# Attention queries and keys: turning by VectorE's 32x32 squares and a round trip through DRAM in place of TensorE transposes

## The chip, the cores and the metric

The kernel runs on one core of one Trainium2 chip. The metric is the device time of one execution in microseconds (us); lower is better. The engines are named as in the profile: PE is TensorE (PEld its weight loads), DVE is VectorE, ACT is ScalarE, POOL is GpSimd, and SP is SyncE, which issues nearly all the DMAs.

## The reference, cut to what matters

The program is a trunk of two layers over 1024 tokens of width 1024. Layer 0 mixes tokens by a gated MLP and a gated delta rule, layer 1 by differential attention; each layer then has an MLP and a gate. Everything is float32. The change concerns the attention of layer 1 alone:

```python
def diff_attention(qkv, q_gain, k_gain, lam_params, sub_gain, lam_init):
    q, k, v = jnp.split(qkv, 3, axis=-1)          # 8 heads, 2 branches of 64 each
    q = rms_norm(q.reshape(bsz, seq, C_HEADS, 2, C_HEAD_DIM), q_gain) * (C_HEAD_DIM ** -0.5)
    k = rms_norm(k.reshape(bsz, seq, C_HEADS, 2, C_HEAD_DIM), k_gain)
    ...
        logits = jnp.einsum('bqhrd,bkhrd->bhrqk', q_blk, k) - slopes * dist
        logits = jnp.where(dist >= 0, logits, -jnp.inf)
        probs = jax.nn.softmax(logits, axis=-1)
        attn = probs[:, :, 0] - lam * probs[:, :, 1]
        return jnp.einsum('bhqk,bkhe->bqhe', attn, v)
```

The projections give q and k with tokens on partitions. The product of q and k sums over features, so both must be turned to features on partitions first.

## The kernel before

The function `attention` works head by head (8 heads, each with two branches of 64 features, so 128 features) and in each head by 8 blocks of 128 queries.

**Projections.** A stream of units (`proj_qk`, `proj_v`) computes q, k and v; each weight is split into a high and a low float32r part (L223 on ACT, L224 on POOL here), and each product takes three matmuls. `proj_qk(hd, qk)` yields, for each of four pairs of token tiles `t2`, a PSUM tile with 256 tokens of q and k. Its `evac` squares it (L914, ACT), reduces it (L916, DVE), takes the power -1/2 (L919, POOL), and `scale` (L923, DVE) writes q and k, normalised, to the SBUF tiles `qk[0]` and `qk[1]`: each a pair of tiles of 128 partitions (tokens) by 4 x 128 (four token tiles by 128 features), one for each half of the sequence. `scale` runs one unit after the `evac` that made it.

**Turning.** `put_k(hf)` turns half `hf` of k by four PE transposes into a PSUM tile `pt`, and writes it from there with the gain to `ks`, as a float32r high part (L969, ACT) and the rest (L970, DVE), for each branch. `put_q(b2)` does the same for 256 queries with two transposes (L980 on ACT, L981 and L982 on DVE). `begin(hd + 1)` calls `put_k(0)` and `put_q(0)` of the next head towards the end of this one; `put_k(1)` follows in the head's own block 2 or 3, and `put_q` before each further pair of blocks.

**Blocks.** For each block and branch, two matmuls give the logits (qk, L76), one DVE operation adds the position term and finds the running minimum (L1016), ACT takes the exponential (L1019), DVE combines the two branches (L1027), PE transposes the result to PSUM (tr), ACT copies it out (aT, L1037), and PE multiplies it with v (po). The outputs go to `o_dram` on SP (L1065).

**The order.** The loop over the blocks runs the steps of three successive blocks beside each other, and calls `pump()` four times for each block; `pump` takes units of the projection stream (and at the end of the output product) by a table of marks. The framework then orders each engine's instructions by a planner that works with estimated times, and sets the waits; every engine takes its queue in that order. Weight loads (L101) go through 8 raw buffers on SP's queue. All PE instructions show as L76 (matmul) or L79 (transpose), as a helper records them.

Of the kernel before, what the change touches and what calls it, by code (L numbers as in the profile page):

```python
# [11 lines left out]
F32 = mybir.dt.float32  # L12
# [6 lines left out]
P = 128  # L19
# [4 lines left out]
HT = 512  # L24
# [15 lines left out]
def f32(ap):  # L40
    return ap.bitcast(F32)
# [73 lines left out]
class Trunk:  # L115
# [756 lines left out]
    def attention(self, w_qkv, w_out, gain_next, h_dram):  # L872

        nc = self.nc
        NB = NT
        hs, r = list(self.hs), list(self.r)
# [16 lines left out]
        def proj(label, srcs, t2s, evac):  # L893
            def units(w):
                for t2 in t2s:
                    ps = self.mm_ps()
                    for i in range(2):
                        h, c = tok(2 * t2 + i)
                        for k in range(KT):
                            self.mm3(ps[:, 256 * i : 256 * (i + 1)], [x[:, c] for x in hs[h][k]], w.at(k), k == 0, k == KT - 1)  # L900
                            if k == 3 or (k == 7 and i == 0):
                                yield None
                    yield evac(t2, ps)

            n = 256 // len(srcs)
            return Proj(label, [(ap, i * n) for i, ap in enumerate(srcs)], 256, units, 4 * len(t2s), nc.gpsimd)

        def proj_qk(hd, qk):
            def evac(t2, ps):
                if not qk:  # L910
                    qk.append([self.slot(f"c{2 * (hd % 2) + i}", [P, 4, P], F32, "q") for i in range(2)])
                    qk.append([self.slot(f"c{4 + i}", [P, 4, P], F32, "k") for i in range(2)])
                sq = self.tmp()
                nc.scalar.activation(sq, ps, AF.Square)  # L914
                ss = self.sp.tile([P, 2, 4], F32, tag="ss", name=self.nm("ss"))
                nc.vector.tensor_reduce(ss, sq.rearrange("p (t g d) -> p t g d", t=2, g=4), AX.X, ALU.add)  # L916
                nc.vector.scalar_tensor_tensor(ss, ss, 1.0 / 64, e2[:, 2 * t2 : 2 * t2 + 2].unsqueeze(2).to_broadcast([P, 2, 4]), ALU.mult, ALU.add)
                f = self.sp.tile([P, 8], F32, tag="ssf", name=self.nm("ssf"))
                nc.gpsimd.tensor_tensor(f, ss.rearrange("p t g -> p (t g)"), self.mhalf[:, 0:8], ALU.pow)  # L919

                def scale():
                    for i in range(2):
                        nc.vector.tensor_tensor(  # L923
                            qk[i][t2 // 2][:, 2 * (t2 % 2) : 2 * (t2 % 2) + 2, :].rearrange("p t (g d) -> p t g d", d=64),
                            ps.rearrange("p (t i g d) -> p t i g d", t=2, i=2, d=64)[:, :, i],
                            f.rearrange("p (t i g) -> p t i g", t=2, i=2)[:, :, i].unsqueeze(3).to_broadcast([P, 2, 2, 64]), ALU.mult)

                return scale

            return proj(f"qk{hd}", [w_qkv[:, i * D + hd * P : i * D + (hd + 1) * P] for i in range(2)], range(4), evac)  # L930
# [25 lines left out]
        def begin(hd):  # L956

            qk = qks[hd]

            ks = self.slot(f"A{2 + hd % 2}", [P, 2, S], F32R, "ks")  # L960

            def put_k(hf):
                pt = self.aux([P, HT], "tr", "tr")
                for t in range(4):
                    self.pe.transpose(pt[:, t * P : (t + 1) * P], qk[1][hf][:, t, :], self.ident)
                for r in range(2):
                    own, other = half[r], half[1 - r]
                    dst = ks[:, r, hf * HT : (hf + 1) * HT]
                    nc.scalar.activation(dst[own], pt[own], AF.Copy, scale=self.kg[own])  # L969
                    nc.vector.scalar_tensor_tensor(dst[other], pt[own], self.kg[own], f32(dst[own]), ALU.mult, ALU.subtract)  # L970

            def put_q(b2):
                pt = self.aux([P, HT], "tr", "tr")
                for i in range(2):
                    self.pe.transpose(pt[:, i * P : (i + 1) * P], qk[0][b2 // 2][:, 2 * (b2 % 2) + i, :], self.ident)
                qh = self.slot(f"c{11 + b2 % 2}", [P, 2, 2 * P], F32R, "qh")
                ql = qlow[b2 % 2]
                for r in range(2):
                    own, other = half[r], half[1 - r]
                    nc.scalar.activation(qh[own, r], pt[own, 0 : 2 * P], AF.Copy, scale=self.qg[own])  # L980
                    nc.vector.tensor_copy(qh[other, r], f32(qh[own, r]))  # L981
                    nc.vector.scalar_tensor_tensor(ql[own, r], pt[own, 0 : 2 * P], self.qg[own], f32(qh[own, r]), ALU.mult, ALU.subtract)  # L982
                return qh, ql

            put_k(0)
            heads[hd] = [ks, put_k, put_q, put_q(0)]

        class Block:
# [105 lines left out]
        qks, vs, os = [[] for _ in range(8)], [], [[] for _ in range(8)]  # L1094

        projs = [proj_v(0, 0, vs), proj_qk(0, qks[0]), proj_v(0, 1, vs)]
        for hd in range(1, 8):
            projs.append(proj_qk(hd, qks[hd]))
            if hd < 7:
                projs.append(proj_v((hd + 1) // 2, (hd + 1) % 2, vs))  # L1100
# [882 lines left out]
```

## Time and profile before

| | |
|---|---|
| runs | 2537.97, 2538.5, 2539.23 us; median 2538.5 us |
| the profiled execution: span | 2535.2 us (its own time is given by the span alone) |
| attention stage, by the windows | about 1260 to 1710 us of the span |
| PE busy | 2515.3 us, 99% |
| VectorE busy | 1854.3 us, 73% |
| ScalarE busy | 1285.9 us, 51% |
| GpSimd busy | 285.5 us, 11% |
| DMA | 396.92 MB, mean 157 GB/s |

The span runs from the first to the last instruction of one profiled execution; the runs' times are of whole executions without a profile. Busy shares are means over stages with different limits, so the stage around the change is looked at by itself. Matmuls overlap, so the distance from one start to the next is what one costs, not its listed duration.

### The profile page before, as it was taken

The page shows a single profiled execution, that of the slowest core. Times are in us where ns is not written, and L with a number is a line of the kernel's source. Part 1 is how long each engine was busy: PE and PEld are TensorE (multiplying, and loading weights), DVE is VectorE, ACT ScalarE, POOL GpSimd, SP SyncE. Part 2 cuts the span into 40 slices and gives each one's busy share as a digit, 9 for nine tenths or more (in the row PEclk, how much of TensorE's full clock was granted, in tenths as well). Part 3 has the DMA queues.
Part 4 walks back from the last instruction along what each step waited for, and adds up shares of the span by engine and source line. Part 5 has one row for each costly group of instructions (what it writes and reads, how often), then busy time and mean ns, then how long its engine had stood idle before and what let it go on. Part 6 is the DMA issues. An engine that isn't in the chain of part 4 may idle for free.

```text
span 2535.2 us, 40147 instructions
## 1 busy us (share of the span) xinstructions
PE 2515.3 (99%) x14046; PEld 2151.9 (85%) x14046; DVE 1854.3 (73%) x3676; ACT 1285.9 (51%) x2553; POOL 285.5 (11%) x256
## 2 busy tenths in 40 slices
PE   9999999999999999999999999999999999999999
PEld 7898898888888878888999999988778888888877
DVE  7867776697666888656477777787887677787586
ACT  6543444465455434544366666665654555445452
POOL 0301232000000000000334333310000000000000
PEclk9999999999999999999999999999999999999999
DMA  7452435457557756553211111147466558655651
GB/s 242 126 157 78 136 110 193 138 175 242 161 174 257 245 164 207 183 158 120 74 53 47 55 47 43 59 136 257 143 219 202 174 184 281 216 184 185 200 178 59
DMA packets 298818, 396.92 MB, mean 157 GB/s; under 512 B 37780, under 2 KB 165752, under 8 KB 298616
## 3 DMA queue, kind: packets, MB, share of 16 engines
q1 hardware_dynamic: 298600, 394.36, 48.4%
q8 instruction: 110, 1.80, 0.3%
q14 instruction: 92, 0.75, 0.1%
q10 hardware_dynamic: 16, 0.00, 0.0%
HBM read 289.40 MB, written 104.86 MB: 156 GB/s over the span
## 4 chain that ended last, share of the span: by engine, by line
PE 92%; DVE 4%; DMA 2%; issue 1%; ACT 1%; SPq 0%; POOL 0%; DVEq 0%; ACTq 0%; POOLq 0%
PE mm L76 79%; PE po L76 3%; PE qk L76 2%; PE aux L76 2%; PE tr L79 2%; DMA raw<-in_w_ple_gate_dram 1%; DVE lg L1016 0%; DVE w L224 0%; DMA raw<-in_w_mlp_dram 0%; PE pz L76 0%; PE py L76 0%; PE aux L79 0%; PE pvn L76 0%; PE pab L79 0%; PE pkq L76 0%
## 5 line engine op out<-in xcount | busy, mean ns | idle before, releaser
L76 PE MATMUL mm<-g,w 128*128 128x512 f32 x2592 | 603.6, 394 | 0.8 <-DVE g L224 0.5
L223 ACT CAST w<-raw 128x512 fp32r<-128x512 f32 x598 | 366.0, 618 | 453.8 <-PE mm L76 386.8
L76 PEld LDWEIGHTS mm<-g,w 128*128 128x128 f32 x2592 | 485.9, 188 | 116.2 <-DVE g L224 1.0
L76 PE MATMUL mm<-hi,w 128*128 128x512 f32 x1728 | 553.6, 396 | 0.3 <-ACT hi L1219 0.3
L76 PE MATMUL mm<-w,hi 128*128 128x256 f32 (+2 forms) x2528 | 505.5, 295 | 0.0
L224 DVE TENSOR_TENSOR w<-raw,w 128x512 fp32r<-128x512 f32 x534 | 364.8, 690 | 178.9 <-ACT w L223 169.4
L76 PEld LDWEIGHTS mm<-w,hi 128*128 128x128 f32 x2528 | 400.1, 188 | 13.6 <-DVE acc L284 0.3
L76 PEld LDWEIGHTS mm<-hi,w 128*128 128x128 f32 x1728 | 324.7, 188 | 73.7 <-ACT hi L1219 0.7
L76 PE MATMUL mm<-w,lo 128*128 128x256 f32 (+2 forms) x1264 | 370.3, 293 | 0.0
L76 PE MATMUL mm<-lo,w 128*128 128x512 f32 x864 | 341.6, 396 | 0.9 <-DVE lo L1220 0.9
L76 PE MATMUL mm<-t,w 128*128 128x512 f32 x1152 | 270.9, 394 | 1.2 <-ACT w L223 1.2
L76 PEld LDWEIGHTS mm<-t,w 128*128 128x128 f32 x1152 | 216.2, 188 | 52.8 <-ACT w L223 1.6
L76 PEld LDWEIGHTS mm<-w,lo 128*128 128x128 f32 x1264 | 238.2, 188 | 5.6
L76 PEld LDWEIGHTS mm<-lo,w 128*128 128x128 f32 x864 | 162.8, 188 | 36.8 <-DVE lo L1220 1.4
L224 DVE TENSOR_TENSOR g<-graw,g 128x512 fp32r<-128x512 f32 x216 | 147.2, 685 | 8.8 <-DMA gd<-g 6.9
L223 ACT CAST g<-graw 128x512 fp32r<-128x512 f32 x216 | 132.7, 617 | 32.8 <-issue 10.9
L1019 ACT ACTIVATE lg<-lg,nm 128x128 f32<-128x128 f32 (+7 forms) x128 | 99.5, 777 | 82.5 <-DVE nm L1016 76.0
L260 POOL TENSOR_TENSOR r<-ms,mhalf 128x4 f32<-128x4 f32 x12 | 13.3, 1109 | 1060.9 <-DVE ms L258 1033.5
L350 ACT ACTIVATE g<-g 128x512 f32<-128x512 f32 x96 | 60.6, 632 | 114.8 <-DVE g L284 114.5
L1016 DVE CUSTOM_DVE_ANT_0 lg<-qk,al 128x512 f32<-128x512 f32 (+3 forms) x128 | 75.1, 589 | 36.2 <-PE qk L76 32.8
L224 POOL TENSOR_TENSOR w<-raw,w 128x512 fp32r<-128x512 f32 x64 | 84.6, 1347 | 111.9 <-ACT w L223 63.0
L76 PE MATMUL mm<-ohi,w 128*128 128x512 f32 x256 | 85.2, 400 | 0.5 <-ACT ohi L1073 0.5
(336 smaller groups left out, 3612.4 us busy)
## 6 DMA issues: line engine op xcount, KB each, us to landing
raw<-in_w_mlp_dram SPq DMA_DIRECT2D x352, 256.0 KB, 3.3
graw<-gd SPq DMA_DIRECT2D x224, 256.0 KB, 2.8
gd<-g SPq DMA_DIRECT2D x192, 256.0 KB, 3.1
raw<-in_w_ple_gate_dram SPq DMA_DIRECT2D x76, 256.0 KB, 3.5
acc<-h_dram SPq DMA_DIRECT2D x64, 256.0 KB, 4.4
keep<-in_w_mlp_dram SPq DMA_DIRECT2D x64, 256.0 KB, 4.3
raw<-in_w_in_e_dram SPq DMA_DIRECT2D x60, 256.0 KB, 3.7
h_dram<-acc SPq DMA_DIRECT2D x48, 256.0 KB, 2.5
```

The source lines that it names most:

```text
L76: self._next(self.engine.matmul(*a, **k))
L79: self._next(self.engine.transpose(*a, **k))
L223: self.nc.scalar.copy(hi, src)
L224: (lo_engine or self.nc.vector).tensor_tensor(lo, src, f32(hi), ALU.subtract)
L260: nc.gpsimd.tensor_tensor(r, ms, self.mhalf[:, 0:4], ALU.pow)
L350: nc.scalar.activation(g, src, AF.Relu)
L1016: nc.vector.tensor_tensor_reduce(out=lg[:, k0:k1], in0=ps[:, : k1 - k0], in1=al[:, u0 + k0 : u0 + k1], scale=-1.0, scalar=3.0e38 if c == 0 ...
L1019: nc.scalar.activation(lg[:, :n], lg[:, :n], AF.Exp, bias=nm[:, r, nch - 1 : nch], scale=-1.0, accum_out=me.sums[:, b, r : r + 1])
```

## The change

When the second `scale` of a half has written a half of q or k, a new function `turn` turns that half in place. VectorE transposes each 32x32 square of the 128 x 512 tile where it stands. The tile is stored to a DRAM buffer, and four loads, one for each quarter of the partitions, bring the squares back to the places that they have in the transposed 128 x 128 tiles; each run in DRAM is 32 numbers, 128 bytes. This happens 32 times: 8 heads, q and k, two halves. `put_k` and `put_q` then read the turned SBUF tile in place of the PSUM tile, and their 128 PE transposes are gone.

```diff
+        def turn(x):
+
+            d = self.dp.tile([4, P, P], F32, name=self.nm("turn"))
+            nc.vector.transpose(x.rearrange("p t d -> p (t d)"), x.rearrange("p t d -> p (t d)"))
+            nc.sync.dma_start(d.rearrange("t p c -> p t c"), x)
+            src = d.rearrange("t (i r) (j c) -> j r t i c", r=32, c=32)
+            for j in range(4):
+                nc.sync.dma_start(x[32 * j : 32 * j + 32].rearrange("p t (i c) -> p t i c", c=32), src[j])
+
         def proj_qk(hd, qk):
...
                             f.rearrange("p (t i g) -> p t i g", t=2, i=2)[:, :, i].unsqueeze(3).to_broadcast([P, 2, 2, 64]), ALU.mult)
+                        if t2 % 2:
+                            turn(qk[i][t2 // 2])
...
             def put_k(hf):
-                pt = self.aux([P, HT], "tr", "tr")
-                for t in range(4):
-                    self.pe.transpose(pt[:, t * P : (t + 1) * P], qk[1][hf][:, t, :], self.ident)
+                pt = qk[1][hf].rearrange("p t c -> p (t c)")
...
             def put_q(b2):
-                pt = self.aux([P, HT], "tr", "tr")
-                for i in range(2):
-                    self.pe.transpose(pt[:, i * P : (i + 1) * P], qk[0][b2 // 2][:, 2 * (b2 % 2) + i, :], self.ident)
+                pt = qk[0][b2 // 2][:, 2 * (b2 % 2) : 2 * (b2 % 2) + 2].rearrange("p t c -> p (t c)")
```

## The prediction

> **What bounds the kernel now.** I read the page first: its span, the busy shares, the chain that ended last.
>
> ```profile
> span 2535.2 us, 40147 instructions
> PE 2515.3 (99%) x14046; PEld 2151.9 (85%) x14046; DVE 1854.3 (73%) x3676; ACT 1285.9 (51%) x2553; POOL 285.5 (11%) x256
> PE 92%; DVE 4%; DMA 2%; issue 1%; ACT 1%; SPq 0%; POOL 0%; DVEq 0%; ACTq 0%; POOLq 0%
> ```
>
> The runs' median is 2538.5 us; the profiled execution spans 2535.2 us, and I take 3.3 us to lie around every span. TensorE (PE) is the bound. The change touches one stage only, the attention, so the second view is the table of windows over it (columns: window, length, then busy us and count of PE, weight loads, VectorE, ScalarE, GpSimd, then the granted clock, DMA share and GB/s), and the third is who PE and VectorE wait for there.
>
> ```profile
> 1262.00:1710.00 448.00, 444.05 (x3472) 427.34 (x3471) 337.21 (x976) 276.04 (x679) 153.89 (x126) 1.00 0.20 63
> PE qk L76 <- DVE nm L1016: 1.5, 2, 0.8
> PE tr L79 <- DVE olo L1074: 1.3, 2, 0.7
> DVE lg L1016 <- PE qk L76: 33.7, 44, 2.8
> ```
>
> In these 448 us PE is busy for 444 and its two longest waits sum to 2.8 us; VectorE is busy for 337 (75%), and what it waits for most is PE's logits (33.7 us). So time taken off PE here should come off the span as long as VectorE, ScalarE and the new transfers keep up.
>
> **What it removes.** The fourth view is the tiles q and k, and then the timeline, for the pitch of a transpose (start, duration, engine, instruction, count).
>
> ```profile
> L79 PE MATMUL tr<-ident,k x64: 270/272/273, 1259.5 to 1695.5; 128*128 128x128 f32 x64
> L79 PE MATMUL tr<-ident,q x64: 270/272/328, 1259.8 to 1704.6; 128*128 128x128 f32 x64
> 1310.09 0.60 PE L79 MATMUL tr<-ident,k 128*128 128x128 f32 x4
> 1310.53 0.38 PE L79 MATMUL tr<-ident,q 128*128 128x128 f32 x2
> ```
>
> 64 + 64 transposes go. Each is listed at 272 ns, but they overlap: four start at 1310.09 and the next instruction at 1310.53, 0.44 us for 4, 0.11 us each. (The 272 ns would give 34.8 us; the pitch counts, since the chain runs from issue to issue.) 128 x 0.11 = **14.1 us off PE**, all on the path. The short PSUM tiles that they filled go too; nothing there is late next, since PE hardly waits.
>
> **What it adds on VectorE.** 32 square transposes of 128x512 (8 heads, q and k, two halves). The nearest row is the same instruction at 128x128; for the length I take another VectorE operation at both widths.
>
> ```profile
> L1644 DVE STREAM_TRANSPOSE inv<-inv x8: 300/311/314, 190.5 to 368.1; 128x128 f32<-128x128 f32 x8
> L1016 DVE CUSTOM_DVE_ANT_0 lg<-qk,al 128x512 f32<-128x512 f32 x76 | 52.3, 689 | 18.9 <-PE qk L76 18.0
> L1016 DVE CUSTOM_DVE_ANT_0 lg<-qk,al 128x128 f32<-128x128 f32 x16 | 4.6, 290 | 1.8 <-PE qk L76 1.1
> ```
>
> From 128 to 512 columns costs 689 - 290 = 399 ns, so 311 + 399 = 0.71 us; the upper bound is 4 x 311 = 1.24 us, the lower 0.69. I take 0.71: 32 x 0.71 = **22.7 us** (22 to 40).
>
> Besides, the second pass of put_k (L970, 32 times) and put_q (L982, 64 times) now reads its first operand from SBUF instead of PSUM, and its third operand already lay in SBUF.
>
> ```profile
> L970 DVE SCALAR_TENSOR_TENSOR ks<-tr,kg,ks x32: 744/751/757, 1267.8 to 1698.7; 64x512 fp32r<-64x512 f32 x32
> L982 DVE SCALAR_TENSOR_TENSOR ql<-tr,qg,qh x64: 469/486/493, 1261.4 to 1708.6; 64x256 fp32r<-64x256 f32 x64
> L981 DVE CAST qh<-qh x64: 277/289/1323, 1261.1 to 1707.8; 64x256 fp32r<-64x256 f32 x64
> L981 DVE CAST qh<-qh 64x256 fp32r<-64x256 f32 x63 | 25.7, 408 | 9.8 <-ACT qh L980 8.6
> L1027 DVE SCALAR_TENSOR_TENSOR lg<-lg,rs,lg 128x896 f32<-128x896 f32 x5 | 6.5, 1298 | 0.1
> L1027 DVE SCALAR_TENSOR_TENSOR lg<-lg,rs,lg 128x1024 f32<-128x1024 f32 x5 | 6.4, 1285 | 0.2
> ```
>
> With PSUM among the inputs these two never vary: 744 to 757 ns, 469 to 493. Operations wholly on SBUF do: L981's median is 289 ns, its mean 408 and its longest 1323, and L1027 takes longer over 896 columns than over 1024. So the new form costs between nothing and L981's excess, 119 ns: at most 96 x 0.119 = 11.4 us. I take two thirds, **8 us**: L970 and L982 stand next to L981 in the queue, so part of the hold-up is met already by L981.
>
> [...]
>
> VectorE then stands at 337 + 22.7 + 8 = 368 us in 448 - 14 = 434, 85%. What of the 30.7 us reaches PE lies between nothing (VectorE had 111 us idle) and all of it. Nearest is today's row: at 75% PE waits 1.5 us for the logits' minimum and 1.3 us for olo. I take as much again, **3 us**. ScalarE's 96 passes only change their source, and it was busy 276 of 448 us: nothing, covered by its idle time.
>
> **The round trip.** Each turn adds a store of 256 KB and four loads of 64 KB on SP's queue, the loads waiting for the store. The rows of the page on issue and landing (last column us to landing) and on issue time:
>
> ```profile
> o_dram<-o SPq DMA_DIRECT2D x14, 256.0 KB, 2.0
> uv_dram<-t SPq DMA_DIRECT2D x14, 256.0 KB, 2.6
> inv<-solved SPq DMA_DIRECT2D x48, 16.0 KB, 1.9
> raw<-in_w_qkv_o_dram SPq DMA_DIRECT2D x64, 128.0 KB, 2.4
> L1640 SPq DMA_DIRECT2D inv<-solved x32: 319/430/1565, 186.0 to 364.6; - x32
> ```
>
> Store: 2.0 to 2.6, I take 2.3 us. Load: inv has the same 128-byte runs but a quarter of the size, raw is larger with longer runs; 1.9 to 2.4, I take 2.2. Issue: 0.43 us each. Bytes are no matter: 32 x 0.5 MB in 434 us is 39 GB/s on top of 63.
>
> Counted from the end of q's scale: q squared at 0.71, k scaled at 1.12, k squared at 1.83. If both stores go out before the loads: q's store lands at 3.0, its loads issue to 4.7; k's store lands at 4.1, its loads issue from 4.7, the last at 6.0, landed at 8.2. k's scale used to end 0.4 us after q's, so k is ready T = 7.8 us after the old end of its scale. If SP takes the turns one after the other, k's store waits behind q's loads: issued 4.7, landed 7.0, last load 8.3, ready 10.5, T = 10.1 us. Now the room that there is, from k's scale of a half (L923) to its first transpose:
>
> ```profile
> 1272.35 0.42 DVE L923 TENSOR_TENSOR k<-mm,ssf 128x256 f32<-128x256 f32 x1
> 1278.84 0.60 PE L79 MATMUL tr<-ident,k 128*128 128x128 f32 x4
> 1302.51 0.41 DVE L923 TENSOR_TENSOR k<-mm,ssf 128x256 f32<-128x256 f32 x1
> 1310.73 0.68 ACT L969 ACTIVATE ks<-tr,kg 64x512 fp32r<-64x512 f32 x1 [0.61 <-PE tr L79]
> 1415.39 0.41 DVE L923 TENSOR_TENSOR k<-mm,ssf 128x256 f32<-128x256 f32 x1
> 1426.52 0.60 PE L79 MATMUL tr<-ident,k 128*128 128x128 f32 x4
> 1532.29 0.41 DVE L923 TENSOR_TENSOR k<-mm,ssf 128x256 f32<-128x256 f32 x1
> 1539.87 0.60 PE L79 MATMUL tr<-ident,k 128*128 128x128 f32 x4
> 1588.26 0.41 DVE L923 TENSOR_TENSOR k<-mm,ssf 128x256 f32<-128x256 f32 x1
> 1596.52 0.60 PE L79 MATMUL tr<-ident,k 128*128 128x128 f32 x4
> ```
>
> ScalarE's first use of k came 0.64 us after the first transpose (1310.73 against 1310.09 above), so the rooms are: head 0's second half 6.1 + 0.6 = 6.7 us; head 1 7.8; head 3 10.7 + 0.6 = 11.3; head 5 7.2 + 0.6 = 7.8; head 6 7.9 + 0.6 = 8.5. Heads 2 and 4 I count as head 3, head 0's first half as head 1; the other second halves have more. At T = 7.8 only head 0's second half is late, by 1.1 us. At T = 10.1: 3.4 + 3 x 2.3 + 1.6 = 11.9 us. A late k holds put_k's copies on ScalarE and VectorE, and behind them in order the exponentials, the weight copies and the logits' evictions, on which PE's own qk matmuls wait; PE has projections to do meanwhile, so I let half land on it: half of the mean of the two (6.5) is **3 us**. SP's own queue is moved past too: weight loads behind a blocked turn start up to 10 us later, covered as SP now stands idle for longer than that, waiting for buffers to come free:
>
> ```profile
> SPq L101 <- POOL w L224: 184.0, 52, 25.7
> ```
>
> **Sum:** -14.1 + 3 + 3 = -8.1 us: a span of 2527.1, runs at **2530.4 us**.
>
> **The rivals.** *VectorE eats it.* If 12 of the 30.7 us land on PE (or the squares take 1.24 us), the sum is -14.1 + 12 + 3 = +0.9: 2539.4 us, no change. For it: the tightest stretches are heads' starts, where squares, put_k and GpSimd's weight parts come together. Against: 111 us of idle VectorE, and PE's short waits.
>
> *The trip does not fit (slower).* One mechanism: the store, its landing and the four loads, all on SP in order, take longer than the rooms. With all lateness on PE it decides from about T = 10: 14.1 - 3 = 11 us of gain against 11.9 us late. At T = 15 (each landing some 2 us longer, as when loads with many short runs or a weight load stand ahead of them) eight turns are late: 8.3 + 3 x 7.2 (head 0's first half, heads 1 and 5) + 6.5 + 3 x 3.7 = 47.5 us; half of it on PE gives -14.1 + 3 + 24 = +13, 2551 us; all of it 2575. For it: the trace has no 64 KB load in 128-byte runs, and 512 of these are four times inv's. Against: 1.9 us for 16 KB is hardly less than 2.4 us for 128 KB, so the size barely shows.
>
> *Short runs are slow.* If the 1.9 us of inv were run time and not fixed, a load of 64 KB takes 7.6 us, four in a row 30 us, and 32 turns 970 us against a stage of 448: some 500 us slower. The same row's nearness to 2.0 us for 256 KB speaks against it. [...]
>
> **How the numbers follow.** The forecast gets 0.54 (it holds from the full 14.1 us, 2524, to 2533), VectorE 0.16, the trip 0.27, short runs 0.03. A measurement of this kernel can tell about 0.2%, 5.1 us, from no change: faster 0.54, same 0.16, slower 0.27 + 0.03 = 0.30. The range starts 1.4 us below the full gain, for waits of PE that go with it, 2523, and reaches past the even case to the trip with half its lateness, 2554. Cases of both signs count; the forecast's own range is 2523 to 2533.
>
> **What would show it.** Right: no PE transposes of q and k, PE still over 98% busy between 1262 and about 1700 us, the stage some 8 us shorter, squares at 0.71 us, VectorE near 85%, L970's longest well over 757 ns, first use of k 8 us after the scale. Wrong: rows of ScalarE or VectorE at put_k waiting for the turn's loads by microseconds, and PE waits of over 10 us in the stage; landings over 4 us; or PE waiting for VectorE's minimum in each head.

## The result, and the profile after

| | before | after |
|---|---|---|
| runs, median (lowest to highest) | 2538.23 us (2537.40 to 2539.23, 4 runs) | 2557.69 us (2556.47 to 2560.86, 4 runs) |
| ratio after / before, 95% interval | | 1.0080 (1.0066 to 1.0094) |
| profiled execution, span | 2535.2 us | 2559.2 us |

The change made the kernel slower by 19.5 us. The forecast was 2530.4 us, and its range ended at 2554. The profiled execution of after ran in 2560.86 us, so 1.7 us lie around its span, less than the 3.3 us that the prediction took.

The page of after, in the lines that answer to those shown of before (span, busy time by engine, chain by engine):

```profile
span 2559.2 us, 40204 instructions
PE 2514.4 (98%) x13918; PEld 2145.8 (84%) x13918; DVE 1889.1 (74%) x3708; ACT 1283.6 (50%) x2553; POOL 289.7 (11%) x256
PE 80%; DVE 9%; DMA 4%; issue 2%; ACT 2%; SPq 1%; POOL 1%; DVEq 0%; ACTq 0%; POOLq 0%
```

PE has its 128 instructions less, but its share of the chain fell from 92% to 80%, and VectorE, DMA and ScalarE took what it lost. PE's busy time hardly fell (2515.3 to 2514.4 us). To see where, the windows of after (columns as in the prediction), then the one of before that the prediction did not show:

```profile
1262.00:1710.00 448.00, 418.95 (x3240) 401.13 (x3239) 357.17 (x965) 264.81 (x654) 156.41 (x123) 0.98 0.36 90
1250.00:1784.00 534.00, 504.36 (x3738) 475.03 (x3738) 410.02 (x1090) 301.65 (x735) 166.45 (x134) 0.99 0.38 104
1270.00:1290.00 20.00, 17.51 (x118) 16.72 (x117) 13.77 (x32) 9.67 (x24) 8.90 (x7) 0.83 0.51 123
```

```profile
1250.00:1760.00 510.00, 505.57 (x3854) 481.49 (x3853) 373.86 (x1058) 303.41 (x735) 162.56 (x134) 1.00 0.24 76
```

Before's 510 us and after's 534 us hold nearly the same work, and the whole loss: the same eight output transposes follow the stage 24.9 us later, against 24.0 us of the span.

```profile
1754.87 1.04 PE L79 MATMUL tr<-ident,o 128*128 128x128 f32 x8
```

```profile
1779.81 1.03 PE L79 MATMUL tr<-ident,o 128*128 128x128 f32 x8
```

In these stretches PE stands idle for 534.00 - 504.36 = 29.6 us after, and 510.00 - 505.57 = 4.4 us before: 25.2 us more. And the clock that PE was granted, as a share of its full speed, is 1.00 over before's stage; here it is 0.99 on average and 0.83 between 1270 and 1290 us (last section). Who holds PE, from the waits of after (1250 to 1760 us; total us, times, longest): first what ScalarE waits for, then PE and VectorE.

```profile
ACT ks L978 <- DMA k<-turn: 22.2, 13, 4.8
ACT qh L987 <- DMA q<-turn: 16.8, 17, 2.1
PE po L76 <- ACT aT L1044: 15.0, 13, 2.1
PE mm L76 <- DVE k L932: 4.2, 3, 1.5
PE mm L76 <- POOL w L224: 3.3, 6, 1.0
DVE ks L979 <- ACT ks L978: 19.3, 7, 5.3
DVE qh L988 <- ACT qh L987: 13.5, 13, 3.0
```

ScalarE stands for 39 us at the copies of `put_k` and `put_q`, waiting for the turn's loads. VectorE then stands behind it at the second pass of the same copies, and PE waits for what both had queued behind these: the turned probabilities (aT), the scale (k) that frees its projection tile, and the weight parts (w), whose low part GpSimd makes from the high part that ScalarE makes. In before the same wait for aT, of PE's po, summed to 0.4 us.

One turn in full, head 1's second half, from the timeline of after, in order of time (start, duration, engine):

```profile
1332.42 0.41 DVE L932 TENSOR_TENSOR k<-mm,ssf 128x256 f32<-128x256 f32 x1
1333.48 0.37 SPq L912 DMA_DIRECT2D turn<-q  x1
1333.56 0.71 DVE L911 STREAM_TRANSPOSE k<-k 128x512 f32<-128x512 f32 x1
1334.29 0.37 SPq L912 DMA_DIRECT2D turn<-k  x1
1335.82 1.92 SPq L915 DMA_DIRECT2D q<-turn  x4
1336.59 0.58 ACT L1044 COPY aT<-tr 128x512 f32<-128x512 f32 x1
1337.83 3.00 SPq L915 DMA_DIRECT2D k<-turn  x4
1341.99 0.73 ACT L978 ACTIVATE ks<-k,kg 64x512 fp32r<-64x512 f32 x1 [4.83 <-DMA k<-turn]
1342.75 0.74 DVE L979 SCALAR_TENSOR_TENSOR ks<-k,kg,ks 64x512 fp32r<-64x512 f32 x1 [4.62 <-ACT ks L978]
1346.24 0.39 PE L76 MATMUL mm<-w,hi 128*128 128x256 f32 x1 [1.02 <-POOL w L224]
```

```profile
1323.05 0.41 DVE L923 TENSOR_TENSOR k<-mm,ssf 128x256 f32<-128x256 f32 x1
1337.98 0.60 PE L79 MATMUL tr<-ident,k 128*128 128x128 f32 x4
1338.78 0.67 ACT L969 ACTIVATE ks<-tr,kg 64x512 fp32r<-64x512 f32 x1
```

The second fence is the same half in before. There the copy to `ks` started 15.3 us after its scale had ended (1323.46 to 1338.78), because its transposes stood that far down PE's queue. In after ScalarE reached the copy 4.3 us after the scale (1332.83 to 1337.17, the end of the aT copy), and stood 4.83 us until its loads had landed: 9.2 us from the scale's end. A room of 15 us was there, enough for the trip; the copy had moved up into it.

This turn has the longest wait. Over all 16 halves of k (8 heads, two each), the first copy started 7.8 to 29.2 us after the scale's end in before (median 13.4) and 7.8 to 11.3 us in after (median 9.0); ScalarE got to it, and began to wait where the load had not landed, at a median of 8.2 us. The first copy of each half of q moved up too, from a median of 15.7 us to 6.4.

### The profile page after: what moved, and what is told of

The parts are those of the page before. It is cut to its first block, busy times and chain, and to the rows that moved or that the text cites. A ratio compares the mean times of both kernels' runs of the same rounds, so it can differ in the third digit from the quotient of the medians.

```text
span 2559.2 us, 40204 instructions
## 1 busy us (share of the span) xinstructions
PE 2514.4 (98%) x13918; PEld 2145.8 (84%) x13918; DVE 1889.1 (74%) x3708; ACT 1283.6 (50%) x2553; POOL 289.7 (11%) x256
## 4 chain that ended last, share of the span: by engine, by line
PE 80%; DVE 9%; DMA 4%; issue 2%; ACT 2%; SPq 1%; POOL 1%; DVEq 0%; ACTq 0%; POOLq 0%
PE mm L76 72%; PE aux L76 2%; DVE lg L1023 2%; DMA turn<-q 1%; PE po L76 1%; SPq L915 1%; DVE lg L1034 1%; DMA k<-turn 1%; DVE ql L989 1%; ACT lg L1026 1%; PE tr L79 1%; POOL ssf L928 1%; DVE ks L979 1%; DMA q<-turn 1%; PE qk L76 1%
## 5 line engine op out<-in xcount | busy, mean ns | idle before, releaser
L76 PE MATMUL mm<-w,hi 128*128 128x256 f32 (+2 forms) x2528 | 511.5, 298 | 7.8 <-DVE k L932 4.2
L224 DVE TENSOR_TENSOR w<-raw,w 128x512 fp32r<-128x512 f32 x534 | 363.5, 688 | 176.2 <-ACT w L223 169.3
L224 DVE TENSOR_TENSOR g<-graw,g 128x512 fp32r<-128x512 f32 x216 | 146.8, 683 | 9.3 <-DMA gd<-g 7.4
L260 POOL TENSOR_TENSOR r<-ms,mhalf 128x4 f32<-128x4 f32 x12 | 13.4, 1115 | 1059.6 <-DVE ms L258 1031.3
L224 POOL TENSOR_TENSOR w<-raw,w 128x512 fp32r<-128x512 f32 x64 | 88.6, 1396 | 149.1 <-ACT w L223 143.4
L76 PE MATMUL po<-v,aT 128*128 128x128 f32 x576 | 77.9, 278 | 15.5 <-ACT aT L1044 15.0
L1023 DVE CUSTOM_DVE_ANT_0 lg<-qk,al 128x512 f32<-128x512 f32 (+3 forms) x128 | 74.2, 581 | 17.8 <-PE qk L76 16.6
```

The source lines that it names most:

```text
L76: self._next(self.engine.matmul(*a, **k))
L224: (lo_engine or self.nc.vector).tensor_tensor(lo, src, f32(hi), ALU.subtract)
L1023: nc.vector.tensor_tensor_reduce(out=lg[:, k0:k1], in0=ps[:, : k1 - k0], in1=al[:, u0 + k0 : u0 + k1], scale=-1.0, scalar=3.0e38 if c == 0 ...
```

## The experiments

All were timed beside before on the same chip; before's median was 2536.54 us beside the first four, 2537.27 beside the next four, 2537.18 beside the last four. Differences below are against the before of the same group; intervals are of the ratio.

**Parts of the change by themselves (first group).** No turn at all, then the squares alone, then the trip alone:

```diff
-                        if t2 % 2:
-                            turn(qk[i][t2 // 2])
```

> Neither PE transposes nor the new turn: q and k are left unturned, put_k and put_q read them from SBUF. The ceiling of the change. Both theories: about 14 us under the kernel before, 2522 to 2526 us; were it not so, the transposes' 0.11 us each would not be on the path. Theory B with its weight on the two SBUF inputs: 2530 us or more.

```diff
-            d = self.dp.tile([4, P, P], F32, name=self.nm("turn"))
-            nc.sync.dma_start(d.rearrange("t p c -> p t c"), x)
-            src = d.rearrange("t (i r) (j c) -> j r t i c", r=32, c=32)
-            for j in range(4):
-                nc.sync.dma_start(x[32 * j : 32 * j + 32].rearrange("p t (i c) -> p t i c", c=32), src[j])
```

> VectorE's squares stay, the store and the four loads are left out, so q and k are turned only inside each square. Theory A (the trip: ScalarE and VectorE stand in order behind copies whose loads have not landed): no such wait is left, the 14.1 us of PE's transposes come off and VectorE's new work costs some 3 us: 2526 to 2531 us. Theory B (VectorE's squares and the copies with two SBUF inputs are what starves PE): 2550 us or more, as in the changed kernel.

```diff
-            nc.vector.transpose(x.rearrange("p t d -> p (t d)"), x.rearrange("p t d -> p (t d)"))
```

> The store and the four loads stay, VectorE's squares are left out. Theory A: nearly all of the loss stays, as each turn is only 0.7 us sooner: 2548 to 2558 us. Theory B: most of the loss goes, 2526 to 2535 us.

| | median us | ratio (95%) | against before |
|---|---|---|---|
| no turn | 2521.33 | 0.9940 (0.9925 to 0.9955) | -15.2 us |
| squares only | 2532.52 | 0.9984 (0.9975 to 0.9994) | -4.0 us |
| trip only | 2553.09 | 1.0067 (1.0052 to 1.0082) | +16.6 us |

The time without the turn lies 0.7 us under its range, that of the squares 1.5 us over theory A's, that of the trip in theory A's. Taking the transposes off PE is worth 15.2 us. Squares in front of the copies give back 11.2 us of that, the trip in front of them 31.8 us and so the sign. With the trip alone ScalarE's waits are like those of the whole change:

```profile
ACT qh L986 <- DMA q<-turn: 21.6, 20, 2.7
ACT ks L977 <- DMA k<-turn: 18.8, 17, 4.3
```

With 40.4 us of such waits the kernel loses 31.8 us against no turn. That is no fixed price of a wait: without the turn ScalarE stands for 18.4 us at the same copies (12.1 for k's scale, 6.3 for q's), and PE, 2.6 us idle between 1250 and 1760 us, hardly notices. With the trip VectorE stands 34.2 us behind those copies, without the turn 5.8. The whole change is set against no turn by the spans and PE's busy times of the profiled executions; the lines of the page without the turn:

```profile
span 2521.2 us, 39884 instructions
PE 2502.5 (99%) x13918; PEld 2140.5 (85%) x13918; DVE 1863.0 (74%) x3676; ACT 1286.4 (51%) x2553; POOL 287.3 (11%) x256
```

Against this the change's span is 38.0 us longer (34.7 by the medians). Of these PE is idle for 26.1 us more, and busy 11.9 us longer over the same 13918 matmuls. Of the 11.9 some 2.6 us are the lower clock, an estimate from its rounded means over the spans (0.997 over 2559.2 us, against 0.998 over 2521.2 without the turn: 0.003 x 2559.2 - 0.002 x 2521.2). The rest is not explained here.

**More room.** The projections run eight units earlier, in the change and then in before.

```diff
-MARKS = ((64, 50), (192, 144), (223, 168))
+MARKS = ((64, 58), (192, 152), (223, 168))
```

> The whole change, with the projections taken 8 units earlier by the table of marks, so that each half of k and q has some 20 us more between its scale and its use. Theory A: the waits at put_k and put_q go and most of the loss with them: 2527 to 2535 us. Theory B: VectorE has the same work, 2553 to 2560 us.

> The kernel before with the projections 8 units earlier, as a control of the earlier units alone. If the earlier units only give room to the turns: the time of the kernel before within 0.3%, 2530 to 2545 us. If earlier units themselves shift work well or badly: outside of it by as much as they moved the changed kernel.

The change with it: 2543.10 us, ratio 1.0026 (1.0014 to 1.0038). Before with it: 2542.99 us, 1.0023 (1.0012 to 1.0034). The first fits neither theory's range: no gain over before, but 12.9 us of the 19.5 us of loss are gone. The marks cost before itself 5.7 us, so measured against its own control the change costs hardly anything here (about 1 us). What the room took away are the waits for q (16.8 us, now 3.3), whose copies now start a median of 17.0 us after their scale. It did not take ScalarE's waits for k away: those copies moved up with the turn. Waits, and the turn of head 2's first half, with these marks:

```profile
ACT ks L978 <- DMA k<-turn: 21.3, 15, 3.5
ACT qh L987 <- DMA q<-turn: 3.3, 3, 1.9
```

```profile
1363.01 0.69 DVE L911 STREAM_TRANSPOSE k<-k 128x512 f32<-128x512 f32 x1
1372.13 0.72 ACT L978 ACTIVATE ks<-k,kg 64x512 fp32r<-64x512 f32 x1 [3.45 <-DMA k<-turn]
```

The waits for k are as long as with the old marks (22.2 us), with eight units more of room: over the 16 halves the first copy of k starts a median of 9.1 us after its scale, 9.0 with the old marks. And 21.3 us of waits for k went with far less loss here, once more without a fixed price.

**The copies held behind PE (second group).** `behind` gives the planner an order and adds no wait: ScalarE's copies are planned behind the PE instruction that stood last when they were written, the place in the program where the transposes used to be. DMAs and VectorE's work stay as in the change.

```diff
-                    nc.scalar.activation(dst[own], pt[own], AF.Copy, scale=self.kg[own])
+                    self.pe.behind(nc.scalar.activation(dst[own], pt[own], AF.Copy, scale=self.kg[own]), self.pe.mark)
...
-                    nc.scalar.activation(qh[own, r], pt[own, 0 : 2 * P], AF.Copy, scale=self.qg[own])
+                    self.pe.behind(nc.scalar.activation(qh[own, r], pt[own, 0 : 2 * P], AF.Copy, scale=self.qg[own]), self.pe.mark)
```

> The whole change; in put_k and put_q ScalarE's copies are held, in the order alone, behind the last PE instruction written before them, so that they stand in the queue where the program has them and not where the planner expects the loads to land. Theory A in its second form (without a PE step in front of them the copies are put as early as the planner believes the loads landed, a few us too soon, whatever the room): the waits on the loads fall from 39 us to under 12 and the time to 2530 to 2540 us. If the room itself is too short (theory A as first stated): 2550 us or more, as in the changed kernel.

Measured: 2532.73 us, ratio 0.9983 (0.9973 to 0.9993), 4.5 us faster than before where the change was 19.5 us slower: the hold is worth 24 us. The time is in the range of theory A's second form; the waits, 14.1 us, are over the 12 that it allowed. Its ScalarE waits, its window, and head 1's second half in it:

```profile
ACT qh L987 <- DMA q<-turn: 7.5, 6, 2.7
ACT ks L978 <- DMA k<-turn: 6.6, 8, 2.5
```

```profile
1262.00:1710.00 448.00, 439.43 (x3388) 420.68 (x3388) 373.99 (x1023) 279.50 (x689) 159.65 (x126) 1.00 0.39 101
```

```profile
1326.70 0.41 DVE L932 TENSOR_TENSOR k<-mm,ssf 128x256 f32<-128x256 f32 x1
1336.51 1.46 ACT L978 ACTIVATE ks<-k,kg 64x512 fp32r<-64x512 f32 x2
```

39 us of waits became 14.1, PE's idle time in the 448 us fell from 29.1 to 8.6 us, and the clock is at 1.00 again, with VectorE busier than in the change (374 against 357 us of the window). In the turn shown the copy starts 9.4 us after the scale's end, and there is no wait in front of it.

The hold did not bring before's places back. Over the 16 halves the first copy of q starts a median of 12.7 us after its scale (6.4 in the change, 15.7 in before), that of k 9.4 us (9.0 and 13.4). For k what differs is what ScalarE did until then: it reached the copy at a median of 9.0 us in place of 8.2, with other work done first. With the trip alone the hold is worth as much (third group), with the squares alone only 4.8 us, although there, without the hold, the copies of k stand closest behind the scale (median 1.8 us). So the loss came from copies that stood in the queues ahead of the landing of their loads; the same trip, copied a little later, costs 24 us less.

**Held, with more room, and k turned first.** Both were to take the remaining 14 us of waits away. In the second the marks move by four units only.

> The copies held as before and the projections 8 units earlier, so both the place and the room are given. Second form of theory A: hardly a wait on the loads is left, and the time is that of the squares alone, 2527 to 2535 us. First form: as with the units earlier alone, about 2543 us.

```diff
-MARKS = ((64, 50), (192, 144), (223, 168))
+MARKS = ((64, 54), (192, 148), (223, 168))
...
-                    for i in range(2):
+                    for i in (1, 0):
```

> The copies held, the projections 4 units earlier, and k turned before q, so that k lands some 2 us sooner. Second form of theory A: 2527 to 2536 us, waits on k's loads under 5 us. First form: 2543 to 2550 us.

Held with eight units: 2537.38 us, 1.0003 (0.9994 to 1.0012), 5.6 us under its control (before with these marks). Hardly a wait at the copies is left (0.9 us), but the time missed its range by 2.4 us; PE waits 6.1 us for VectorE's minimum (nm) there, 2.2 in the change. Held with four units and k first: **2527.69 us, 0.9961 (0.9946 to 0.9975)**, 9.6 us faster than before, the best version that does the whole computation, with time and waits as its expectation had them. Its waits for the turn and its window:

```profile
ACT ks L978 <- DMA k<-turn: 0.5, 2, 0.3
ACT qh L987 <- DMA q<-turn: 0.4, 1, 0.4
```

```profile
1262.00:1710.00 448.00, 442.35 (x3404) 423.01 (x3404) 379.09 (x1034) 282.24 (x695) 162.00 (x129) 1.00 0.40 102
```

**What remains when the copies are held (third group).** The hold with the squares alone (the store and loads left out, as above), and with the trip alone (the squares left out):

> The copies held, VectorE's squares kept, the store and the loads left out. What the squares cost once nothing is put too early: if the 11 us between squares alone and no turn were again copies placed too early, 2521 to 2526 us; if they are VectorE's time, 2529 to 2534 us as without the hold.

> The copies held, the store and the loads kept, the squares left out. What the trip costs once its loads are waited for in the right place: 2521 to 2527 us if the waits were all of its price, 2535 us or more if the 32 stores and 128 loads on SP's queue or the DMA engines have a price of their own.

Squares: 2528.40 us, 0.9967 (0.9954 to 0.9979), -8.8 us. Trip: 2529.34 us, 0.9970 (0.9960 to 0.9981), -7.8 us. Each fell between the ranges of its two cases. Against the 15.2 us of no turn the squares still cost 6.4 us and the trip 7.4; both together cost 10.7 us, with intervals of some 3 us on each. Without the hold they cost 11.2 and 31.8. No turn with the hold was not run, so part of what remains may be the hold itself.

The two parts of the best version by themselves: held and k first with the old marks, and before with the marks four units earlier.

> The copies held and k turned before q, with the units where they were. Parts the best version so far: if k first is what brings it, 2526 to 2530 us; if the units 4 earlier do, 2531 to 2535 us.

> The kernel before with the projections 4 units earlier: the control of the best version. If the units alone gain nothing there: 2535 to 2541 us. If they gain by themselves, 2527 to 2533 us, and the best version owes its time to them and not to the turning.

Held and k first: 2535.25 us, 0.9995 (0.9985 to 1.0004), 2.5 us above held alone (in another group), and 0.3 us above the higher of its ranges. Before with the marks: 2539.51 us, 1.0007 (0.9998 to 1.0016), as expected if the units gain nothing by themselves. Neither gains alone. In the traces, k first without the marks keeps 9.4 us of waits for k, and PE waits 7.7 us for VectorE's minimum; the first copy of k starts a median of 8.9 us after its scale. With the marks it starts at 17.4 us: held copies do take up the room that the marks give, as the free ones did not. What the best version gains over held comes from the two together, or from the marks with the hold; held with four units without k first was not run, so this stays open.

## Why the prediction was wrong, step by step

- **PE's 14.1 us** were right: no turn gained 15.2 us, its span 14.0. The pitch was the price, not the listed 272 ns (34.8 us).
- **The squares** were right in size: 0.71 us each foretold, 0.70 and 0.68 measured, 22.0 us in all.

```profile
L911 DVE STREAM_TRANSPOSE q<-q 128x512 f32<-128x512 f32 x16 | 11.2, 703 | 0.0
L911 DVE STREAM_TRANSPOSE k<-k 128x512 f32<-128x512 f32 x16 | 10.8, 676 | 0.0
L989 DVE SCALAR_TENSOR_TENSOR ql<-q,qg,qh 64x256 fp32r<-64x256 f32 x64 | 34.3, 536 | 1.4
L979 DVE SCALAR_TENSOR_TENSOR ks<-k,kg,ks 64x512 fp32r<-64x512 f32 x32 | 28.2, 883 | 20.2 <-ACT ks L978 19.3
```

```profile
L982 DVE SCALAR_TENSOR_TENSOR ql<-tr,qg,qh 64x256 fp32r<-64x256 f32 x64 | 30.9, 483 | 1.6
L970 DVE SCALAR_TENSOR_TENSOR ks<-tr,kg,ks 64x512 fp32r<-64x512 f32 x32 | 24.0, 750 | 1.9 <-ACT ks L969 0.9
```

- **The copies from SBUF**: 8 us foretold; the groups of after and before give 34.3 + 28.2 - 30.9 - 24.0 = 7.6 us.
- **What VectorE's load does to PE** was mis-sized: 3 us foretold for squares and copies together; the squares alone, against no turn, cost 11.2 us without the hold and 6.4 with it. Without the hold that is nearly the rival in which VectorE eats the gain (12 us). Not all of it is VectorE's load, since the hold took 4.8 us of it away.
- **The trip's length** came out at the long end of the forecast. The medians to landing, from the DMA list of after, are 0.3 us over the forecast's terms (2.3 for the store, 2.2 for a load); q's are 2.3 and 2.3:

```profile
turn<-k SPq DMA_DIRECT2D x16, 256.0 KB, 2.6
k<-turn SPq DMA_DIRECT2D x64, 64.0 KB, 2.5
```

  Both stores went out ahead of the loads in all 16 halves. The last load of k landed 8.5 to 11.1 us after its scale, 9.8 on average, where 7.8 to 10.1 were foretold. (The first copy needs only two of the four loads and could start at 9.2 in the turn shown.) So the rival of short runs did not happen (a 64 KB load was to take 7.6 us). The rival of the trip that does not fit had the sign right for another reason: at 9.8 us the prediction's own rooms make 3.1 + 3 x 2.0 + 1.3 = 10.4 us of lateness, which even wholly on PE gives no loss of 19.5 us, and its T = 15 was not seen.
- **The rooms were the step that failed.** They were read from before, from the scale to the old copy, as though the copy would stay there. Its place had been set by the PE transposes ahead of it, in PE's full queue. The change took these away, and the copies then needed only ScalarE, VectorE and the loads. They moved up to 4.3 us behind the scale where the old room was 15.3, so even the halves with "more" room came late, and 22.2 us of waits for k alone took the place of the 6.5 us foretold. The rooms of q were not reckoned at all; its waits brought 16.8 us more. Held behind PE, the same trip fitted in most places (14.1 us of waits, 6.6 of them for k; 4.5 us faster than before, against the 8.1 us foretold).
- **Half of the lateness on PE** was too little here: with the trip alone 40.4 us of waits went with 31.8 us of loss. ScalarE and VectorE stood together, and PE stood at po for aT (15.0 us in after); what follows po in its queue began only behind it (at the longest of these waits, 2.08 us, po started at 1531.85 and the next projection matmul at 1532.10). A share that holds for every run does not exist, as no turn and the earlier units show.

That the planner put the copies up because it reckoned the loads to land earlier than they do is inferred: its own times are in no trace. Shown is that the copies moved up, that they waited there (k's also where there was more room), and that an order alone brought 24 us back.

## What to carry to other kernels

The instructions taken off one engine had also set the place of their followers in the other engines' queues (in the turn shown the copy started 15.3 us behind the scale with them, 9.2 without). Before a room is read from an old trace, ask what holds the follower there, and whether the change removes that; if it does, give the follower an order of its own, late enough for the slower path. A wait on an engine that is not the bound had no price of its own here (18.4 us of ScalarE's waits at the copies without the turn left PE 2.6 us idle, 40.4 us with the trip alone went with 31.8 us of loss); ask what stands behind it in the queues, and whether the bound needs that soon. And when a transfer's own length is as foretold but the time is not, look for engines that stand at its consumer (here ScalarE, for 39 us), before shortening the transfer.

## What was not expected of the hardware

The granted clock of PE fell to 0.50 behind three of its short pauses in the stage. At head 0's first blocks, from the timeline and the windows of after:

```profile
1271.78 0.41 PE L76 MATMUL mm<-w,hi 128*128 128x256 f32 x2
1272.14 0.40 PE L76 MATMUL mm<-w,hi 128*128 128x256 f32 x2
1273.70 0.33 PE L76 MATMUL qk<-ks,qh 128*128 128x128 f32 x1 [0.70 <-DVE ks L979]
1277.06 0.77 PE L76 MATMUL mm<-w,hi 128*128 128x256 f32 x2 [1.54 <-DVE k L932]
1279.12 0.63 PE L76 MATMUL mm<-w,hi 128*128 128x256 f32 x2
1279.76 0.63 PE L76 MATMUL mm<-w,hi 128*128 128x256 f32 x2
```

```profile
1276.00:1284.00 8.00, 6.94 (x36) 6.97 (x37) 4.33 (x17) 2.58 (x9) 1.36 (x2) 0.57 0.58 136
```

The same group of matmuls starts every 0.36 us before the pauses, every 0.64 us behind them, and every 0.36 again from 1283.21 us; between 1270 and 1290 us the granted clock is 0.83. From 1277.06 to 1282.97 us PE ran at the longer distance: an estimate of 5.91 x (1 - 0.36 / 0.64) = 2.6 us lost, beside the 2.5 us of standing. The clock was at 0.50 from 1276.15 to 1282.97 us, and twice more in the stage, for 3.4 us each (from 1347.83 and 1532.15); in the windows of the stage around and between these it was 1.00. In the 3.41 us ahead of the three, about the length of the two shorter stretches, PE was busy for 1.83, 1.69 and 1.33 us. But with 1.72 us of 3.40, from 1460.50, the clock stayed at 1.00, as it did at PE's other pauses in the stage. So three stalls of PE were paid for twice here, and the others were not; what parts them is not shown.

With both inputs in SBUF, the second pass of `put_k` (L979) keeps its median of 750 ns and has a mean of 883. In after its six long ones (943 to 1670 ns) all began while GpSimd was making a weight part (L224); the other ten that ran beside GpSimd took at most 780 ns, and the 16 that ran beside no GpSimd instruction took 744 to 751. In before, with PSUM among its inputs, none was longer than 757 ns, though 22 ran beside GpSimd. L981, which reads a single SBUF tile, was slower beside GpSimd as well (617 ns on average in before, 288 elsewhere).
